# A hybrid stick-breaking and retention step on one core: DRAM read-backs and 32x32 transposes of the first group bound to products in the schedule, the sample row finished apart, value panels moved

## The chip, the cores and the metric

The kernel runs on one core of a Trainium2 chip. The metric is device time of one execution in microseconds (us), the median of several runs. All times of the trace are microseconds from the start of the profiled execution's span. Engines are named as the profile does it: PE multiplies matrices (PEld loads its stationary operand), DVE and ACT are the vector and the scalar engine, POOL is GpSimd, SP only issues DMAs. SPq, ACTq and POOLq are the queues on which an engine issues DMAs.

## What is computed

One layer of a hybrid step over 1,024 prompt rows and a sample of 8 running streams with 16 rows each (128 rows, "the sample row tile"), width 2,048, all in float32:

```python
h = rms_norm(x, norm_pre)
q_sb, k_sb, v_sb, gate_sb, q_r, k_r, v_r, gate_r = split(h @ w_in)    # 8 x 1024 columns, 8 heads of 128
# A: stick-breaking attention, strictly causal
z = q_sb @ k_sb.T / sqrt(128)
log_keep = where(strict, log_sigmoid(-z), 0)
a = where(strict, exp(log_sigmoid(z) + reversed_cumsum(log_keep) - log_keep), 0)
o_sb = a @ v_sb               # sample rows: over 1024 cached keys and values of their stream, then their own
# B: retention with rotary q and k, per-head decay, a state carried over chunks
o_r = decayed(q_r @ k_r.T) @ v_r + decay_read * (q_r @ S);  S = gamma^n * S + (decay_write * k_r).T @ v_r
y = concat(head_rms_norm(o_sb) * silu(gate_sb), head_rms_norm(o_r) * silu(gate_r))
x = x + rms_norm(y @ w_out, norm_post)
```

Outputs are the rows, the new keys and values, and the retention states, for prompt and sample.

## The kernel before

**Products.** Each float32 operand is split into a high part and a rest (`split`, L126: ACT writes the high part `wh`, DVE subtracts to get `wl`), and each product is three matmuls (high x high, high x rest, rest x high). The normed rows stand in SBUF as `mh`, `ml` (the moving operand); the weights stream through: SP loads a 128x512 tile (`wr`), ACT and DVE split it, PE uses it. `wp`, the pool of these tiles, has 4 buffers. A "product" below is one matmul of L206 or L252 (L225 and L274 in the changed file).

**Groups and heads.** The rows are handled in two groups: group 0 holds prompt tiles 0 to 3 and the sample tile (5 tiles of 128 rows, in pieces of 256 and 384), group 1 holds prompt tiles 4 to 7 (one piece of 512). For each of 8 heads the main loop (from L803) emits the projections in this order: `project` of column blocks 4 (retention q) and 5 (retention k), every second head `project_rows` of block 6 (retention v of two heads, "the value panel"), `project` of 7 (retention gate), 0 and 1 (stick-breaking q and k), every second head `project_rows` of 2 (v of two heads), `project` of 3 (gate). After both groups the output projection follows (`out_panel`).

**Side work.** All else is done by generators wrapped in `Job`: `ret_branch` (retention of a head), `sb_branch` (stick-breaking of its prompt rows), `decode` (its sample rows, over the cache). After each product step `tick()` advances one job by one step if its time has come; the number a generator yields is how many ticks it then waits. These numbers are the table `D_*` (first value: group 0, second: group 1). `drain(job)` ticks until a job is done, with no product between the steps. In this way the order of the program is written; a scheduler of the framework then arranges each engine's instructions by that order and the dependences it knows. Names with a number (`wr_10573`) are buffers of the schedule.

**Turning through DRAM.** A block matrix is transposed in two halves: `turn_out` writes it to DRAM (`s_be` and `s_bd` for the weights of stick-breaking of prompt and sample rows, `s_rk` for retention keys, `s_o` for a finished head), `turn_in` (L438) reads it back with the 32x32 blocks in transposed places by four DMAs, and a DVE `transpose` then turns every 32x32 block. Between the halves a job waits `D_TO` ticks (for stick-breaking rows `D_TB` and the steps of the next row), between read-back and transpose `D_TI`.

- `stick_breaking` (L515): step s issues the read-back of row s-1 (POOL's queue) first, then transposes row s-2 (L525), then computes scores, sigmoids and weights of row s and writes them out, then multiplies row s-2 with `vn` (L559).
- `decode` (L566): loads the cached keys of the head in 16 pieces (`kc`, L585, POOL's queue), transposes each on DVE (L610), multiplies; loads the cached values in 8 pieces of 512 KB (`vc`, L616, SP's queue). `kcT` and `vc` share 5 buffers (`V_BUFS`), so piece k+5 is loaded once the matmuls of piece k (L648) are issued. Its last steps copy and combine the accumulator `pa` into tile 4 of `so` on DVE (L654, L656).
- `pa` is the one buffer of the PSUM pool `psa`, shared by L559, L641, L648 and the retention outputs L686, L691.
- `sb_branch` waits at L796 until `decode` is done, then finishes all 5 tiles of the head (`Out.finish`: norm, `turn_out`, `turn_in`, transpose L504, times gate, store to `s_y`).

Of the kernel before, what the change touches and what calls it, by code (L numbers as in the profile page):

```python
# [34 lines left out]
D_NAT = (14, 11)  # L35
# [9 lines left out]
D_TO = (26, 23)  # L45
D_TB = (33, 33)
D_TI = (12, 13)
# [9 lines left out]
def tile_hybrid_step(  # L57
# [88 lines left out]
    phase = [0]  # L146

    class Job:
        def __init__(self, steps, after=0):
            self.steps, self.at, self.done = steps, clock[0] + after, False  # L150
            jobs.append(self)

    def tick():
        clock[0] += 1
        for job in jobs:
            if job.at <= clock[0]:
                wait = next(job.steps, None)
# [43 lines left out]
    def products(mov, acc, pieces, w, wh, wl):  # L201
        hi, lo = mov
        for j in range(WQ):
            for n, (lhs, rhs) in enumerate(((wh, hi), (wh, lo), (wl, hi))):
                for a, (o, m) in zip(acc, pieces):
# [6 lines left out]
                    )  # L212
                tick()
# [15 lines left out]
    def project_rows(g, mov, col, dst, off):  # L229
# [5 lines left out]
        for w in range(KT // 2):  # L235
# [4 lines left out]
            )  # L240
            wh = wp.tile([P, 2, 2 * P], F32R, name="whn", tag="wh")
            wl = wp.tile([P, 2, 2 * P], F32R, name="wln", tag="wl")
            split(wh, wl, wr)
            for j in range(2):
                q, jj = divmod(2 * w + j, WQ)
                for t in range(nt):
                    a = banks[t // 2][:, t % 2, :]
                    ts = slice(t * P, (t + 1) * P)
                    for n, (lhs, rhs) in enumerate(((hi, wh), (hi, wl), (lo, wh))):


                        nc.tensor.matmul(  # L252
# [13 lines left out]
    with ExitStack() as s1:  # L266
# [29 lines left out]

        def ret_inputs(g, mov, h, acc):
            rq = rope(acc, "rq", *ropes)
            rk = rope(project(g, mov, col(5, h)), "rk", *ropes)
            if h % 2 == 0:  # L300
                pair["r"] = ep.tile([P, 5, 2, P], F32, name="rv", tag="rv")
                project_rows(g, mov, col(6, h), pair["r"], 0)
            rv = pair["r"][:, :, h % 2, :]
            return rq, rk, rv, gate(project(g, mov, col(7, h)), "rg")
# [9 lines left out]
        with tc.tile_pool(name="p0", bufs=2) as p0, tc.tile_pool(name="p0s", bufs=1) as p0s, tc.tile_pool(  # L314
# [90 lines left out]
            first = ret_inputs(g0, mov, 0, list(zip(acc, g0["pieces"])))  # L405
            drain(job)
# [31 lines left out]
        def turn_in(s, raw, q):  # L438

            for i in range(4):  # L440
                q.dma_start(  # L441
                    raw[32 * i : 32 * i + 32, :].rearrange("p (k a) -> p k a", a=32),
                    s[:, :, 32 * i : 32 * i + 32].rearrange("k (j b) a -> b (k j) a", b=32),
                )
# [37 lines left out]
        class Out:  # L482
            def __init__(self, g, tag):
                nt = len(g["tiles"])
                self.g, self.nt = g, nt
# [7 lines left out]
            def finish(self, b, h, gT, oT, dst):  # L493
# [4 lines left out]
                s = turn_out(self.o, f"s_o{b}_{h}_{self.nt}")  # L498
# [5 lines left out]
                nc.vector.transpose(oT[:, :n], flat)  # L504
# [10 lines left out]
        def stick_breaking(g, h, out, q2, k2, rest):  # L515
# [3 lines left out]
            for step in range(len(todo) + lag):  # L519
                if 0 < step <= len(todo):  # L520
                    _, be, turned = rows[step - 1]
                    turn_in(turned, be, nc.gpsimd)
                if step >= lag:
                    kp, be, _ = rows[step - lag]
                    nc.vector.transpose(kp[:, : be.shape[1]], be)  # L525
                if step < len(todo):
# [3 lines left out]
                    for s, w in z_pieces(n):  # L530
# [11 lines left out]
                        yield D_ZP[phase[0]]  # L542
                    yield D_TB[phase[0]]
# [525 lines left out]
```

## Time and profile before

| | us |
|---|---|
| runs, median (lowest to highest) | 2468.1 (2465.5 to 2471.39) |
| the profiled execution, own time | 2463.17 |
| its span in the trace | 2461.1 |
| PE busy in the span | 2367.9 |

The profiled execution is one whole run; it lies 4.9 us under the median, and 2.1 us of its own time lie outside the span. PE is busy for 96% of the span. The stages by time: until about 150 us the rows are normed and turned and the first products start; group 0 runs to about 1,120 us; the change of groups, where the side work of group 0's last head meets the first projections of group 1, to about 1,240 us; group 1 to about 2,020 us; then the rest of the output projection. A row of the windows gives, for each engine, busy us with the number of instructions, then the clock that was granted to PE (1.00 is full), the share of the DMA engines' time, and GB/s. A row of the waits gives the waiting engine and line, what released it, the total us, how often, and the longest.

### The profile page before, as it was taken

What the parts mean: (1) busy time and instruction counts of PE and PEld (TensorE: products, weight loads), DVE (VectorE), ACT (ScalarE), POOL (GpSimd) and SP (SyncE); (2) the same over time, 40 slices, a digit from 0 to 9 for tenths busy, and PEclk for the clock granted to TensorE, in tenths of its full rate; (3) what the DMA queues carried; (4) which work ended last, traced back from release to release, by engine and by line L of the source; (5) the groups of instructions that cost most, each with busy time, mean ns of one, the idle gap of its engine ahead of it and who ended that gap; (6) DMA issues with size and microseconds to landing.
All of it is one profiled execution on the core that took longest, in us unless ns stands there. A gap on an engine that the chain in (4) does not pass through costs nothing.

```text
span 2461.1 us, 40322 instructions
## 1 busy us (share of the span) xinstructions
PE 2367.9 (96%) x14832; PEld 2099.4 (85%) x14832; DVE 1250.0 (51%) x2362; ACT 903.8 (37%) x1913; POOL 641.9 (26%) x1029
## 2 busy tenths in 40 slices
PE   7999899999999999998799999999999998999998
PEld 7999888989898888988578898889889886878787
DVE  8245454454444454444545544554564555564544
ACT  6323232333233232233334434344344443444333
POOL 3244354443433344333402111120220211000000
PEclk9999999999999999999999999999999998999999
DMA  7769677695948678495955655665564566665553
GB/s 241 165 144 210 143 191 173 173 199 140 212 125 221 149 177 178 130 226 146 209 161 150 153 152 142 144 163 135 153 160 128 152 152 170 224 221 191 184 184 133
DMA packets 673094, 418.65 MB, mean 170 GB/s; under 512 B 223744, under 2 KB 617984, under 8 KB 670464
## 3 DMA queue, kind: packets, MB, share of 16 engines
q1 hardware_dynamic: 523760, 285.99, 45.9%
q0 software_dynamic: 32256, 71.36, 12.5%
q10 hardware_dynamic: 116880, 58.74, 8.6%
q8 instruction: 116, 1.90, 0.3%
q14 instruction: 82, 0.67, 0.1%
HBM read 336.24 MB, written 79.69 MB: 169 GB/s over the span
## 4 chain that ended last, share of the span: by engine, by line
PE 75%; DMA 10%; issue 9%; DVE 4%; POOL 1%; ACT 1%; SPq 0%; ACTq 0%; DVEq 0%; POOLq 0%
PE acc L206 38%; PE accn L252 14%; PE a L890 4%; PE a L891 4%; PE a L889 4%; PE pa L559 2%; DMA vc<-cache_sb_v 2%; PE z L535 2%; DMA wr<-w_in 1%; PE zc L601 1%; DMA ro<-s_rk 1%; DMA kc<-cache_sb_k 1%; DMA s_rk<-rk 1%; PE pa L648 1%; DMA s_be<-be 1%
## 5 line engine op out<-in xcount | busy, mean ns | idle before, releaser
L206 PE MATMUL acc<-ml,wh 128*128 128x256 f32 (+2 forms) x2304 | 677.0, 343 | 0.2 <-DVE ml L128 0.2
L206 PE MATMUL acc<-mh,wh 128*128 128x256 f32 (+2 forms) x2304 | 670.5, 341 | 6.5 <-ACT rv L262 3.8
L206 PE MATMUL acc<-mh,wl 128*128 128x256 f32 (+2 forms) x2304 | 669.9, 341 | 3.7 <-DVE wl L128 3.7
L128 DVE TENSOR_TENSOR wl<-wr,wh 128x512 fp32r<-128x512 f32 (+1 forms) x576 | 394.7, 691 | 503.5 <-ACT wh L127 498.5
L127 ACT ACTIVATE wh<-wr 128x512 fp32r<-128x512 f32 (+1 forms) x576 | 356.6, 625 | 730.4 <-PE acc L206 367.9
L206 PEld LDWEIGHTS acc<-mh,wh 128*128 128x128 f32 x2304 | 425.3, 189 | 51.3 <-issue 14.3
L206 PEld LDWEIGHTS acc<-mh,wl 128*128 128x128 f32 x2304 | 425.1, 189 | 47.6 <-issue 12.2
L206 PEld LDWEIGHTS acc<-ml,wh 128*128 128x128 f32 x2304 | 422.5, 190 | 40.3 <-issue 12.4
L585 POOL DMA_DIRECT2D kc<-cache_sb_k x512 | 331.4, 653 | 367.8 <-DVE kcT L610 167.5
L252 PE MATMUL accn<-whn,mh 128*128 128x256 f32 x1152 | 332.5, 289 | 0.0
L252 PE MATMUL accn<-wln,mh 128*128 128x256 f32 x1152 | 326.9, 284 | 3.8 <-DVE wln L128 3.8
L252 PE MATMUL accn<-whn,ml 128*128 128x256 f32 x1152 | 326.5, 284 | 0.0
L252 PEld LDWEIGHTS accn<-whn,mh 128*128 128x128 f32 x1152 | 221.2, 192 | 12.9 <-issue 10.8
L890 PE MATMUL a<-wl,mh 128*128 128x512 f32 (+1 forms) x576 | 221.2, 384 | 7.7 <-DVE wl L128 7.7
L252 PEld LDWEIGHTS accn<-wln,mh 128*128 128x128 f32 x1152 | 221.3, 192 | 7.0 <-DVE wln L128 5.5
L252 PEld LDWEIGHTS accn<-whn,ml 128*128 128x128 f32 x1152 | 221.0, 192 | 1.7 <-issue 1.7
L891 PE MATMUL a<-wh,ml 128*128 128x512 f32 (+1 forms) x576 | 220.5, 383 | 0.0
L889 PE MATMUL a<-wh,mh 128*128 128x512 f32 (+1 forms) x576 | 219.3, 383 | 1.0 <-DVE sg L279 0.6
L890 PEld LDWEIGHTS a<-wl,mh 128*128 128x128 f32 x576 | 109.3, 190 | 31.3 <-DVE wl L128 10.6
L127 ACT ACTIVATE whn<-wrn 128x512 fp32r<-128x512 f32 x128 | 79.8, 634 | 151.2 <-PE acc L206 39.8
L441 POOL DMA_DIRECT2D be<-s_be x128 | 94.1, 741 | 142.4 <-DMA s_be<-be 124.0
L128 DVE TENSOR_TENSOR wln<-wrn,whn 128x512 fp32r<-128x512 f32 x128 | 86.8, 687 | 83.4 <-ACT whn L127 82.8
(184 smaller groups left out, 2602.4 us busy)
## 6 DMA issues: line engine op xcount, KB each, us to landing
wr<-w_in SPq DMA_DIRECT2D x384, 256.0 KB, 3.8
wr<-w_out SPq DMA_DIRECT2D x184, 256.0 KB, 3.6
wrn<-w_in SPq DMA_DIRECT2D x128, 256.0 KB, 3.1
kc<-cache_sb_k POOLq DMA_DIRECT2D x512, 64.0 KB, 4.3
vc<-cache_sb_v SPq DMA_DIRECT2D x64, 512.0 KB, 8.7
xt<-x_prompt SPq DMA_DIRECT2D x8, 1024.0 KB, 6.1
xr<-x_prompt SPq DMA_DIRECT2D x8, 1024.0 KB, 6.0
out<-out ACTq DMA_DIRECT2D x12, 512.0 KB, 2.9
```

Of the source, the lines that this page charges most:

```text
L127: nc.scalar.activation(hi, src, AF.Copy)
L128: nc.vector.tensor_tensor(lo, src, hi.bitcast(F32), ALU.subtract)
L206: last = nc.tensor.matmul(a[:, :m], lhs[:, j, :], rhs[w][:, j, o : o + m], start=(w == 0 and j == 0 and n == 0), stop=(w == KT // WQ - 1 a ...
L252: nc.tensor.matmul(a, lhs[q][:, jj, ts], rhs[:, j, :], start=(w == 0 and j == 0 and n == 0 and t % 2 == 0), stop=(w == KT // 2 - 1 and j = ...
L441: q.dma_start(raw[32 * i : 32 * i + 32, :].rearrange("p (k a) -> p k a", a=32), s[:, :, 32 * i : 32 * i + 32].rearrange("k (j b) a -> b (k ...
L535: nc.tensor.matmul(z[:, :c], q2[a][:, i * P : (i + 1) * P], k2[b][:, s : s + c], start=(m == 0), stop=(m == 2),)
L559: nc.tensor.matmul(po[:, :P], at[:, j, :], vn[:, j, :], start=(j == 0), stop=(j == t))
L585: nc.gpsimd.dma_start(kc[32 * i : 32 * i + 32, :].rearrange("p (k d) -> p k d", d=32), cache_k[0, 2 * c + j, s * 512 : (s + 1) * 512, h, 3 ...
L601: nc.tensor.matmul(z[r, :], qp[:, j, r], ready[c // 2][:, c % 2, :], start=(j == 0), stop=(j == 1))
L889: nc.tensor.matmul(a[:, :width], hi[q][:, j, ts], wh, start=(k == 0), stop=False)
L890: nc.tensor.matmul(a[:, :width], hi[q][:, j, ts], wl, start=False, stop=False)
L891: nc.tensor.matmul(a[:, :width], lo[q][:, j, ts], wh, start=False, stop=(k == KT - 1))
```

## The change

It is confined to the side work and to where two kinds of projection panel stand.

1. `tied()` adds, in group 0 only, a dependence for the scheduler alone (no semaphore) from each read-back DMA and each transpose after a read-back to the product that was emitted last (`anchor`).
2. Spacing of group 0: `D_NAT` 14 to 8, `D_TO` 26 to 32, `D_TB` 33 to 17 with a new `D_TA` of 14 ahead, `D_TI` 12 to 32. In `stick_breaking` the read-back of row s-1 moves behind the scores of row s. A job keeps the phase in which it was made, so that group 0's jobs keep their numbers when they run on into group 1.
3. The sample row gets an `Out` of its own (`do`, 128x128) and a job of its own for its finish (norm, write-out, read-back, 128x128 transpose, gate); the finish of the prompt rows covers 4 tiles and no longer waits for `decode`. A `drain(sub)` stands ahead of the next head's `decode` instead.
4. The retention value panel (block 6) moves to the end of the odd head before; in group 1 the panel of head 0 comes first and takes over the loads of its moving rows. `ret_branch` starts ahead of the gate projection 7 and waits for the gate only at its finish.

```diff
-D_NAT = (14, 11)
+D_NAT = (8, 11)
...
-D_TO = (26, 23)
-D_TB = (33, 33)
-D_TI = (12, 13)
+D_TO = (32, 23)
+D_TA = (14, 0)
+D_TB = (17, 33)
+D_TI = (32, 13)
...
+    def tied(ins):
+
+        if phase[0] == 0 and anchor[0] is not None:
+            tc.add_manual_dep(
+                ins.ins,
+                anchor[0].ins.name,
+                mybir.DependencyInfo(mybir.DependencyClass.NoSync, mybir.DependencyReason.SCHED_ONLY),
+                reason="tied to the products",
+            )
...
+                anchor[0] = last
                 tick()
...
-                        nc.tensor.matmul(
+                        anchor[0] = nc.tensor.matmul(
...
+        def ret_values(g, mov, h, loads=None):
+            pair["r"] = ep.tile([P, 5, 2, P], F32, name="rv", tag="rv")
+            project_rows(g, mov, col(6, h), pair["r"], 0, loads)
...
         def turn_in(s, raw, q):
 
             for i in range(4):
-                q.dma_start(
...
+                tied(
+                    q.dma_start(
...
-                nc.vector.transpose(oT[:, :n], flat)
+                tied(nc.vector.transpose(oT[:, :n], flat))
...
-                if 0 < step <= len(todo):
-                    _, be, turned = rows[step - 1]
-                    turn_in(turned, be, nc.gpsimd)
+                early = D_TA[phase[0]] == 0
+
+                def read_back():
+                    if 0 < step <= len(todo):
+                        _, be, turned = rows[step - 1]
+                        turn_in(turned, be, nc.gpsimd)
+
+                if early:
+                    read_back()
                 if step >= lag:
                     kp, be, _ = rows[step - lag]
-                    nc.vector.transpose(kp[:, : be.shape[1]], be)
+                    tied(nc.vector.transpose(kp[:, : be.shape[1]], be))
...
                         yield D_ZP[phase[0]]
+                if not early and step <= len(todo):
+                    yield D_TA[phase[0]]
+                    read_back()
                     yield D_TB[phase[0]]
...
-        def decode(h, out, qs, rest):
+        def decode(h, qs, rest):
             i = 4
+            out = Out(1, "do")
...
-            out.done(i)
+            out.done(0)
+            while "sg" not in rest:
+                yield 3
+            last_row = slice(4 * P, 5 * P)
+            oT = op.tile([P, P], F32, name="doT", tag="doT", bufs=1)
+            Job(out.finish(0, h, rest["sg"][:, last_row], oT, s_y[0][h][:, last_row]))
...
-            while "sg" not in rest or sub is not None and not sub.done:
+            while "sg" not in rest:
...
-                    acc = project(g, mov, col(4, h), loads, (0, 1))
-                    loads = None
+                    if h == 0:
+                        ret_values(g, mov, h, loads)
+                        loads = None
+                    acc = project(g, mov, col(4, h))
                     drain(ret_job)
-                    inputs = ret_inputs(g, mov, h, acc)
+                    inputs = *ret_inputs(g, mov, h, acc), {}
                 ret_job = Job(ret_branch(gi, g, h, *inputs), D_NAT[phase[0]])
+                if "rg" not in inputs[-1]:
+                    inputs[-1]["rg"] = gate(project(g, mov, col(7, h)), "rg")
...
-                out = Out(g, "so")
+                out = Out(4, "so")
                 rest = {}
-                sub = Job(decode(h, out, qs, rest), D_DEC) if SAMPLE in tiles else None
+                if SAMPLE in tiles:
+                    drain(sub)
+                    sub = Job(decode(h, qs, rest), D_DEC)
...
+                if h % 2 and h < H - 1:
+                    ret_values(g, mov, h + 1)
```

How the order of instructions moves is shown at three places. In the rows stand the line in the file concerned, the operation, and destination<-sources.

The first is SP's queue where head 5 of group 0 passes into head 6. `wr` and `wrn` are weights, `vc` the cached values of `decode`, `ro<-s_rk` the read-back of the retention keys, `so<-s_o0` that of the finished stick-breaking tiles. Before:

```order
L441 DMA ro_10779<-s_rk0_6_10781 32x20x32
L616 DMA vc_10421<-cache_sb_v 128x8x128
L616 DMA vc_10469<-cache_sb_v 128x8x128
L192 DMA wr_10645<-w_in 128x4x128
L616 DMA vc_10511<-cache_sb_v 128x8x128
L192 DMA wr_10697<-w_in 128x4x128
L192 DMA wr_10734<-w_in 128x4x128
L192 DMA wr_10768<-w_in 128x4x128
L192 DMA wr_10806<-w_in 128x4x128
L441 DMA ro_10779<-s_rk0_6_10781 32x20x32 x2
```

After:

```order
L654 DMA vc_10738<-cache_sb_v 128x8x128
L654 DMA vc_10768<-cache_sb_v 128x8x128
L211 DMA wr_11100<-w_in 128x4x128
L654 DMA vc_10792<-cache_sb_v 128x8x128
L466 DMA ro_10686<-s_rk0_6_10688 32x20x32 x4
L466 DMA so_9439<-s_o0_5_4_0_10714 32x16x32 x4
L211 DMA wr_11151<-w_in 128x4x128
L211 DMA wr_11192<-w_in 128x4x128
```

The four read-backs of the keys, scattered before, stand together and are followed by the four of the finished tiles; between `wr_11100` and the next weights lie nine DMAs.

The second is DVE where head 6 passes into head 7: L765 (L808 after) transposes the retention keys that were read back, L654 and L656 (L692 and L694) empty the accumulator of `decode`. Before:

```order
L610 STREAM_TRANSPOSE kcT_12573<-kc_12568 128x512
L765 STREAM_TRANSPOSE rkn_12344<-ro_12345 128x640
L279 TENSOR_TENSOR rg_12275<-rg_12275,acc0_12122 128x256
L279 TENSOR_TENSOR rg_12275<-rg_12275,acc1_12123 128x384
L128 TENSOR_TENSOR wl_12406<-wr_12403,wh_12405 128x512
L767 TENSOR_SCALAR rkn_12344<-rkn_12344,dec_76 128x128
L654 COPY so_10878<-pa_12045 128x128
```

After:

```order
L808 STREAM_TRANSPOSE rkn_12278<-ro_12279 128x640
L713 TENSOR_TENSOR sc_12512<-rs_12510,dT_12508 128x128
L810 TENSOR_SCALAR rkn_12278<-rkn_12278,dec_76 128x128
L812 TENSOR_SCALAR rkn_12278<-rkn_12278,dec_76 128x512
L811 TENSOR_SCALAR rkn_12278<-rkn_12278,dec_76 128x128
L648 STREAM_TRANSPOSE kcT_12759<-kc_12754 128x512
L713 TENSOR_TENSOR sc_12547<-rs_12545,dT_12508 128x128
L692 COPY do_11046<-pa_12285 128x128
```

In both the copy out of `pa` stands behind the transpose of the keys. What moved is what the copy is combined into (`do`, a tile of its own, for `so`), and that score rows of the retention (L713) and a piece of cached keys (L648) stand between the two, where gate and weights stood.

The third is PE at the change of groups, where the last pieces of `decode` of head 7 (`vc`) meet the first projections of group 1. Before:

```order
L206 MATMUL acc0_13711<-mh0_12778,wl_13715 128x512
L206 MATMUL acc0_13711<-mh1_12851,wh_13741 128x512
L206 MATMUL acc0_13711<-ml1_12852,wh_13741 128x512
L206 MATMUL acc0_13711<-mh1_12851,wl_13742 128x512
L648 MATMUL pa_13544<-vc_13641,kp_12464 32x256 x4
L206 MATMUL acc0_13711<-mh1_12851,wh_13741 128x512
L206 MATMUL acc0_13711<-ml1_12852,wh_13741 128x512
```

After:

```order
L225 MATMUL acc0_13888<-mh1_13039,wl_13935 128x512
L686 MATMUL pa_13805<-vc_13842,kp_12643 32x256 x4
L744 MATMUL pS_13921<-rv_13106,rkn_13771 128x128
L711 MATMUL rs_13944<-rq_13640,rk_13739 128x128
L744 MATMUL pS_13960<-rv_13106,rkn_13771 128x128
L686 MATMUL pa_13805<-vc_13867,kp_12643 32x256
L711 MATMUL rs_13973<-rq_13640,rk_13739 128x128
L744 MATMUL pS_13995<-rv_13106,rkn_13771 128x128
L686 MATMUL pa_13805<-vc_13867,kp_12643 32x256 x3
L686 MATMUL pa_13805<-vc_13902,kp_12643 32x256 x4
L729 MATMUL pa_13909<-rv_13106,sc_13882 128x128
L734 MATMUL pa_13909<-S_13878,rq_13640 128x128
```

Before, products stand on both sides of a piece (nine between it and the piece ahead); after, the last three pieces and the retention of group 1's head 0 (L711, L744, L729, L734) follow one another without a product.

More of the change, by code (lines that the diff above doesn't have):

```diff
@@ L146, in tile_hybrid_step, with step @@
     phase = [0]
+    anchor = [None]
+    def tied(ins):
[6 more added lines that the diff above has]
+            )
+    def step(job):
+        now, phase[0] = phase[0], job.phase
+        wait = next(job.steps, None)
+        phase[0] = now
+        return wait
     class Job:
@@ L156, in tick @@
             if job.at <= clock[0]:
-                wait = next(job.steps, None)
+                wait = step(job)
                 jobs.remove(job)
@@ L240, in project_rows @@
             )
+            for _ in range(WQ if loads and w in (0, 2) else 0):
+                next(loads)
             wh = wp.tile([P, 2, 2 * P], F32R, name="whn", tag="wh")
```

51 lines of the change are left out of this document (28 added, 23 removed).

## Prediction

> **What bounds the kernel now.** I read the page's head first, then the windows by stage, then the waits of PE in each stage, then what the releasers themselves waited for.
>
> ```profile
> span 2461.1 us, 40322 instructions
> PE 2367.9 (96%) x14832; PEld 2099.4 (85%) x14832; DVE 1250.0 (51%) x2362; ACT 903.8 (37%) x1913; POOL 641.9 (26%) x1029
> ```
>
> The windows (PE is the first pair of busy us and count):
>
> ```profile
> 0.00:150.00 150.00, 134.63 (x991) 132.42 (x992) 77.74 (x177) 70.60 (x127) 42.02 (x64) 0.99 0.72 195
> 150.00:1120.00 970.00, 935.23 (x6810) 853.59 (x6809) 463.87 (x931) 294.34 (x655) 398.50 (x666) 0.99 0.77 174
> 1120.00:1240.00 120.00, 106.41 (x656) 91.13 (x655) 66.08 (x128) 45.80 (x99) 40.27 (x68) 0.94 0.74 181
> 1240.00:2020.00 780.00, 779.18 (x4445) 678.08 (x4444) 410.93 (x732) 312.59 (x649) 127.94 (x200) 1.00 0.58 148
> 2020.00:2461.00 441.00, 412.43 (x1938) 344.20 (x1936) 231.43 (x396) 180.47 (x385) 33.21 (x32) 0.98 0.60 189
> ```
>
> PE bounds it; no other engine passes 51%. The change adds no product, so time can come only from PE's idle time and its clock. PE's idle time by stage is the window less the busy time: 15.4 us at the start, 34.8 in group 0, 13.6 at the change of groups, 0.8 in group 1, 28.6 at the end. The start and the end hold nothing that the change ties or spaces, and group 1 has 0.8 to give. So the question is what becomes of 34.8 and 13.6. The waits of PE in group 0 (waiting line, releaser, total us, times, longest):
>
> ```profile
> PE pa L559 <- DVE so L656: 12.2, 4, 7.5
> PE pa L648 <- DMA vc<-cache_sb_v: 9.8, 5, 4.0
> PE acc L206 <- ACT rv L262: 3.8, 2, 2.3
> PE acc L206 <- DVE wl L128: 3.6, 2, 2.1
> PE zc L601 <- DVE kcT L610: 2.9, 3, 1.6
> PE acc L206 <- ACT vn L262: 1.4, 2, 1.1
> PE pa L641 <- DVE kp L635: 1.1, 1, 1.1
> ```
>
> and at the change of groups its two longest:
>
> ```profile
> PE rs L668 <- DVE rk L290: 5.1, 1, 5.1
> PE accn L252 <- DVE wln L128: 3.0, 1, 3.0
> ```
>
> The first seven add up to 34.8, the whole idle time of group 0. The largest is not what its name says. L656 is a 0.34 us instruction; its longest wait, 7.5 us, looks like this on DVE (first two rows) and PE (third; in square brackets the idle time ahead and its releaser):
>
> ```profile
> 1114.26 0.84 DVE L765 STREAM_TRANSPOSE rkn<-ro 128x640 f32<-128x640 f32 x1 [6.48 <-DMA ro<-s_rk]
> 1117.65 0.34 DVE L656 SCALAR_TENSOR_TENSOR so<-pa,dec,so 128x128 f32<-128x128 f32 x1
> 1118.14 1.62 PE L559 MATMUL pa<-vn,kb 128*128 128x128 f32 x6 [7.47 <-DVE so L656]
> ```
>
> DVE stood 6.48 us on a read-back, the copy that frees `pa` stood behind it in DVE's order, and PE behind that copy. How often DVE stands on read-backs in group 0, and how long a read-back takes (us to landing, last column of the rows of DMAs):
>
> ```profile
> DVE kb L525 <- DMA kb<-s_be: 48.2, 12, 6.0
> DVE rkn L765 <- DMA ro<-s_rk: 14.7, 4, 6.5
> ```
>
> ```profile
> wr<-w_in SPq DMA_DIRECT2D x384, 256.0 KB, 3.8
> vc<-cache_sb_v SPq DMA_DIRECT2D x64, 512.0 KB, 8.7
> s_rk<-rk ACTq DMA_DIRECT2D x8, 320.0 KB, 6.2
> ro<-s_rk SPq DMA_DIRECT2D x32, 80.0 KB, 6.2
> ```
>
> The two groups of waits are 62.9 us on DVE, most hidden, since PE has products to go on with. Idle time is paid a second time through the clock:
>
> ```profile
> 263.40:266.80 3.40, 3.40 (x20) 3.09 (x13) 1.00 (x4) 0.00 (x0) 0.00 (x0) 0.50 1.20 183
> 826.60:830.00 3.40, 0.79 (x7) 0.64 (x6) 3.20 (x10) 0.14 (x1) 0.88 (x2) 1.00 0.67 129
> 830.00:833.40 3.40, 3.40 (x17) 3.40 (x16) 1.22 (x5) 0.41 (x3) 1.58 (x3) 0.50 0.51 116
> 833.40:836.80 3.40, 3.40 (x25) 3.40 (x24) 1.28 (x5) 2.81 (x7) 0.99 (x2) 1.00 0.32 68
> 1113.30:1123.50 10.20, 5.36 (x23) 5.39 (x24) 5.64 (x18) 1.20 (x7) 2.39 (x4) 0.50 0.38 89
> ```
>
> After a 3.4 us stretch in which PE was busy for 0.79, the next ran at 0.50 (17 matmuls) and the one behind it at full clock (25). 3.4 us at half clock cost at most 1.7; I take 1.6. Between 150 and 1,120 us five such stretches stand (the first and the last are shown) and the one at 1113.3, where half of 5.36 busy us, 2.7, is lost: 5 x 1.6 + 2.7 = 10.7 us.
>
> [...]
>
> **The change part by part.**
>
> *Ties and spacing (parts 1 and 2).* In the order, a product being one matmul, the read-back of the keys stands 15 to 106 products behind its write-out before, by the head, and 48 behind it in each head after; the transposes then follow another 16 to 66 behind the last read-back (9 to 44 before). The rows that turn products into time:
>
> ```profile
> 681.75 18.48 PE acc L206 x126
> 1401.85 23.87 PE acc L206 x104
> ```
>
> 0.147 us in group 0, 0.230 in group 1. Fifteen products are 2.2 us, less than the 6.2 us of `s_rk` above, so there the read-back was issued too early and SP waited in it; 48 are 7.1 us, more than 6.2. A gap of 16 to 66 products is 2.3 to 9.7 us against the 6.2 us of the second half, so short gaps still stall DVE, but for the difference only, and the copy of L656 behind waits for that much. Of 12.2 us I leave 1 (bounds: 0, as in group 1, whose whole idle time is 0.8; 12.2 if landings drift as much as spacing grew). The 3.6 on `wl` is DVE late for the same reason: 1 left. The 2.9 on `kcT` waits for `kc` loads from POOL's queue, which still carries 64 KB pieces and read-backs: 2.9 left (0 to 6). The transpose `kp` of the sample row now stands 10 products (1.5 us) ahead of its use: 1.1 becomes 3 (0 to 7 x 1.1 = 8).
>
> *Cached values.* The 9.8 us on `vc` fell where pieces 5 to 7 were issued 15 to 20 products (2.2 to 2.9 us) ahead of use, in heads 0 and 1; the other heads had 67 and more (9.8 us, over the 8.7 to landing). After, head 0 has 30, 41 and 52 products (4.4, 6.0, 7.6 us), heads 1 to 6 have 70 to 88. Three pieces short by up to 4.3, 2.7 and 1.1, where an earlier wait delays the later ones: 3 us left (0 to 8). Head 7 is told below.
>
> *Sample row alone (part 3).* 9 DVE and 4 ACT instructions and 4 read-backs more in each head. The nearest row is L656 above, 128x128, 0.34 us: 9 x 0.34 = 3.1 us of DVE per head of about 120, beside DVE at 48% in this stage. Hidden by products; with that cover gone (a stall of DVE in which PE waits for `wl`) it would cost up to 3.1 x 8 = 24. I take 0. The prompt finish, no longer behind `decode`, starts earlier: this frees `so`, which no PE wait names.
>
> *Value panels and the gate (part 4).* The same matmuls and loads in another place. The 3.8 + 1.4 us on `rv`, `vn` are PE waiting while ACT empties PSUM banks; the panels keep that form: 5.2 left (3 to 8). SP carries the panel's loads past other jobs' read-backs; its weights stay 75 and more products ahead of use (11 us against 3.8 to land), 13 to 51 once, where head 0 passes into head 1. That place may cost up to 2 us; 0 taken.
>
> Group 0: 1 + 3 + 1 + 2.9 + 5.2 + 3 = 16.1, from 34.8: -18.7. Of the six half-clock stretches two stay (head 0's `vc`, one at large), 3 of 10.7: -7.7.
>
> *Change of groups.* Here the order speaks against the change. Three pieces of `decode` of head 7 (L686 on `vc`) are loaded 16, 4 and 0 products ahead of use, where nine products stood between them before; behind them the four steps of the retention of group 1's head 0 follow without a product, each through the one `pa` buffer. What such a step is made of, and what a bare `vc` queue looked like here:
>
> ```profile
> L686 PE MATMUL pa<-rv,sc 128*128 128x128 f32 x64 | 12.3, 275 | 0.0
> L695 DVE SCALAR_TENSOR_TENSOR ro<-pa,dec,ro 128x128 f32<-128x128 f32 x32 | 11.1, 348 | 14.2 <-ACT ro L694 13.8
> ...
> L694 ACT ACTIVATE ro<-pa 128x128 f32<-128x128 f32 x32 | 8.9, 278 | 28.6 <-PE pa L691 28.6
> ```
>
> ```profile
> 1192.90 11.94 SPq L616 DMA_DIRECT2D vc<-cache_sb_v  x5
> ```
>
> The pile: 8.7 for the last `vc` to land, less 16 x 0.230 = 3.7 of products; DVE's copy and two combinations, 3 x 0.34 = 1.0; four steps of two matmuls (0.275 each), L694 (0.278) and L695 (0.348), 1.2 each, 4.7 in all; the next weights' split stands behind the last L694 on ACT, 0.3 at least. Sum 11.0. At the least the loads land as the pile's own matmuls run, 3; at the most all three queue as the five did in 11.94 us and the chain follows whole, 20. I take 11. Of the old 13.6, 9 stay (the `rk` and `wln` waits belong to heads' starts that are kept): 20 for 13.6, +6.4. The longer pile brings one more half-clock stretch, +1.6.
>
> Group 1 and the output panels have almost the same order: 0, within 3 either way. Sum: -18.7 - 7.7 + 6.4 + 1.6 = -18.4 on the profiled execution, 2463.2 to 2444.8. That execution lies 4.9 under the median, so the median to expect is 2449.7; I say 2449.
>
> **The rivals.**
>
> *Smaller gain.* A tie holds the order of a list, no time: with the DMA engines 0.77 busy in group 0 landings spread; those of `ro`, least, median and most:
>
> ```profile
> DMA to landing us min/median/max: 1.9/3.7/13.2
> ```
>
> A transpose whose data comes late still blocks DVE. If half of the two largest waits and of the clock stay, 11 of the 26.4 us are not gained: about 2460. [...]
>
> *The change of groups eats it.* With the pile at its upper end of 20 (+9), clock for two more stretches (+3), and 7 of the gain unrealized: 2468, no change.
>
> *Slower: weights starve behind a run of DMAs on SP.* In each steady head nine DMAs now stand between two weight loads on SP, seen in the order, eight of them read-backs that wait for a write-out to land. SP is in order, and the next weights are used 187 products after the first of those `vc`, 27.5 us. The run decides when it takes longer than 27.5 less 3.8 to land, 23.7 us. What such waits cost SP before:
>
> ```profile
> SPq L441 <- DMA s_bd<-be: 41.0, 7, 9.9
> ```
>
> ```profile
> 1100.21 8.31 SPq L441 DMA_DIRECT2D ro<-s_rk  x4
> ```
>
> Two fours at 8.31 (last row) and one wait of 9.9 are 26.5, over the limit by 2.8; with the mean wait, 41.0/7 = 5.9, they are 22.5 and under it. A stall of 2.8 us with 1.7 of clock in each of seven heads is +32 on the expected time: about 2481. Against it: the four `ro` here were issued into a write-out barely begun, and after the change write-outs are 48 products old.
>
> *More gain.* If `rv`, `kp` and the change of groups cost nothing extra, 8 to 15 us more: 2436.
>
> **How the numbers follow.** A difference of 0.2%, 4.9 us, is about what a measurement of this kernel can tell from none. The forecast (2440 to 2457): 0.53. Smaller gain (2457 to 2463): 0.17. No change (2463 to 2473): 0.13. Slower (above 2473, about 2481): 0.11. More gain (under 2440): 0.06. Faster: 0.53 + 0.17 + 0.06 = 0.76; same 0.13; slower 0.11. The range leaves out the slower case and half of "more gain": 2434 to 2472. The forecast's own range is 2440 to 2457.
>
> **What would show it.** In the trace after: PE's idle time in group 0 near 16 us, the wait on L656's successor (L694) near 1, on `vc` near 3 and only in head 0; no more than two or three stretches at 0.50 there; at the change of groups a run of waits of 5 to 12 us at L686 and L729 with a half-clock stretch behind it; group 1 as it was; SP's weights never named by PE. Wrong it would be if PE waits for `wl` with SP as the root in steady heads, if L525's successor blocks DVE in more than a few heads, or if the pile at the change of groups exceeds 20 us.

## The result, and the profile after

| | before | changed |
|---|---|---|
| median of 7 runs, us | 2469.2 (2464.6 to 2474.4) | 2454.13 (2446.88 to 2463.56) |
| ratio to before | | 0.994, 95% interval 0.9921 to 0.9959 |
| profiled execution, own time | 2463.17 | 2452.19 |

The change gains 15 us, 0.6%; 19 were forecast. The head of the page and the windows, the last one shorter since the span is:

```profile
span 2450.5 us, 40488 instructions
PE 2372.9 (97%) x14832; PEld 2100.2 (86%) x14832; DVE 1263.9 (52%) x2434; ACT 915.1 (37%) x1931; POOL 655.6 (27%) x1029
```

```profile
150.00:1120.00 970.00, 959.98 (x7047) 880.62 (x7047) 489.48 (x1038) 324.74 (x712) 410.23 (x681) 1.00 0.84 178
1120.00:1240.00 120.00, 105.88 (x626) 81.69 (x626) 61.16 (x118) 43.81 (x86) 33.30 (x57) 0.95 0.81 184
1240.00:2020.00 780.00, 766.41 (x4275) 665.62 (x4274) 412.90 (x721) 300.18 (x634) 145.48 (x206) 0.99 0.59 146
2020.00:2450.00 430.00, 406.38 (x1917) 340.40 (x1916) 222.83 (x384) 176.20 (x378) 28.67 (x25) 0.98 0.60 188
```

PE's idle time in group 0's window falls from 34.8 to 10.0 us. In group 1's it rises from 0.8 to 13.6, which the prediction did not have. Windows of fixed times cut the two programs at different work, though. Both issue the same 10,368 product matmuls, so I cut both traces at the same counts: a stage ends where the first product behind a head's gate projection 3 starts. All stage times below are taken so.

| stage | before | changed | difference |
|---|---|---|---|
| until the first product | 22.4 | 25.9 | +3.5 |
| group 0 | 1143.6 | 1110.1 | -33.5 |
| head 0 of group 1 (change of groups) | 156.1 | 163.6 | +7.5 |
| heads 1 to 7 of group 1 | 700.5 | 712.9 | +12.4 |
| from there to the last matmul of the output | 428.2 | 427.7 | -0.5 |

Most of the first row isn't the change: the traces of the twelve runs below give 21.6 to 25.0 us, with this part of the program untouched in all. The rows add up to -10.6 us and the two profiled executions differ by 11.0, where the medians differ by 15.1. Stage times of group 0 with the same instructions there (the changed kernel, e1, e2) lie between 1110.1 and 1113.1, so 3 us is about what a stage of one trace can tell.

The waits of PE in group 0 and, in a second fence, at the change of groups:

```profile
PE acc L225 <- DVE wl L129: 3.2, 2, 2.5
PE pa L729 <- DVE do L694: 3.1, 3, 2.3
PE pa L686 <- DMA vc<-cache_sb_v: 1.5, 2, 1.3
PE zc L639 <- DVE kcT L648: 0.7, 1, 0.7
PE pa L596 <- DVE kb L556: 0.5, 1, 0.5
```

```profile
PE pa L596 <- DVE kb L556: 3.8, 2, 2.5
PE accn L274 <- ACT mh L128: 2.9, 2, 1.8
PE acc L225 <- ACT wh L128: 1.9, 2, 1.8
PE pa L729 <- DVE do L694: 1.8, 1, 1.8
PE pS L744 <- DVE rkn L812: 1.1, 1, 1.1
PE pa L686 <- DMA vc<-cache_sb_v: 1.0, 1, 1.0
```

In group 0 the 12.2 us behind L656 have become 3.1 behind L694, its successor, the 9.8 on cached values 1.5, and the 5.2 on emptied value panels are gone. At the change of groups the forecast pile is there, smaller and spread over more names (6.5 us of waits from 1226.5 to 1243.4 us). Its end on PE:

```profile
1227.62 0.64 PE L686 MATMUL pa<-vc,kp 128*32 128x256 f32 x8 [1.05 <-DMA vc<-cache_sb_v]
...
1239.28 0.79 PE L729 MATMUL pa<-rv,sc 128*128 128x128 f32 x2 [0.75 <-DVE ro L738]
...
1241.25 0.80 PE L729 MATMUL pa<-rv,sc 128*128 128x128 f32 x2 [0.75 <-DVE ro L738]
...
1243.36 0.80 PE L225 MATMUL acc<-mh,wh 128*128 128x512 f32 x1 [0.89 <-ACT wh L128]
```

Cached values, then retention steps about 2 us apart, each waiting for the tile ahead to leave `pa`, then the weights' split on ACT; the clock is at half from 1237.2 to 1247.4:

```profile
1237.20:1247.40 10.20, 7.71 (x22) 5.91 (x23) 4.53 (x17) 6.30 (x20) 0.00 (x0) 0.50 0.22 66
```

The loss in group 1 recurs in each odd head at the same place. On ACT (the first three rows) and PE (the others, not all of its rows), at head 1:

```profile
1369.23 0.36 ACTq L533 DMA_DIRECT2D s_y<-rg  x1
1369.62 1.05 ACTq L825 DMA_DIRECT2D out<-kn  x2
1371.59 1.28 ACT L485 ACT_TABLE_LOAD   x1 [4.47 <-DMA out<-kn]
1371.17 0.34 PE L566 MATMUL z<-kh,ql 128*128 128x384 f32 x1
1372.05 0.29 PE L566 MATMUL z<-kh,ql 128*128 128x256 f32 x1
1372.17 0.39 PE L566 MATMUL z<-kh,qh 128*128 128x512 f32 x1
1373.81 0.39 PE L566 MATMUL z<-kh,qh 128*128 128x256 f32 x1 [0.78 <-ACT be L486]
1376.65 0.50 PE L225 MATMUL acc<-mh,wl 128*128 128x512 f32 x1 [1.04 <-DVE wl L129]
```

The same place of the kernel before, at head 3:

```profile
1600.41 0.34 PE L535 MATMUL z<-kh,ql 128*128 128x384 f32 x1
1600.83 1.28 ACT L459 ACT_TABLE_LOAD   x1 [3.25 <-PE z L535]
1601.28 0.29 PE L535 MATMUL z<-kh,ql 128*128 128x256 f32 x1
1601.41 0.39 PE L206 MATMUL acc<-mh,wh 128*128 128x512 f32 x1
```

The store of the finished retention tiles (`s_y<-rg`) now stands between the four stores of keys on ACT, and ACT is idle for longer ahead of the table load. That is not the loss: in both kernels the table load starts 0.08 us after the scores that its sigmoids read (PE's rows of 384 columns). What differs is PE's own order. Before, 12 products follow the score piece of 256 columns; after, the next row's pieces follow at once, and the second of them has to wait until ACT, behind its table load, is through with the first piece's sigmoids. The weights' split comes late as well. In the four odd heads the two waits come to 7.3 us, and the half-clock stretches behind two of them to 3.4, of the 12.4.

### The profile page after: what moved, and what is told of

The parts are those of the page before. It is cut to its first block, busy times and chain, and to the rows that moved or that the text cites. A ratio compares the mean times of both kernels' runs of the same rounds, so it can differ in the third digit from the quotient of the medians.

```text
span 2450.5 us, 40488 instructions
## 1 busy us (share of the span) xinstructions
PE 2372.9 (97%) x14832; PEld 2100.2 (86%) x14832; DVE 1263.9 (52%) x2434; ACT 915.1 (37%) x1931; POOL 655.6 (27%) x1029
## 4 chain that ended last, share of the span: by engine, by line
PE 70%; issue 12%; DMA 8%; DVE 6%; POOL 2%; ACT 1%; SPq 1%; DVEq 0%; ACTq 0%; POOLq 0%
PE acc L225 33%; PE accn L274 15%; PE a L944 4%; PE a L945 4%; PE a L943 4%; PE pa L596 2%; DMA kc<-cache_sb_k 2%; DMA wr<-w_in 1%; PE z L566 1%; PE zc L639 1%; POOL kc L623 1%; DMA mr<-s_y 1%; PE pa L686 1%; DMA ro<-s_rk 1%; DVE wl L129 1%
## 5 line engine op out<-in xcount | busy, mean ns | idle before, releaser
L225 PE MATMUL acc<-mh,wl 128*128 128x256 f32 (+2 forms) x2304 | 661.5, 340 | 7.4 <-DVE wl L129 7.4
L225 PE MATMUL acc<-ml,wh 128*128 128x256 f32 (+2 forms) x2304 | 666.8, 342 | 0.0
L225 PEld LDWEIGHTS acc<-mh,wh 128*128 128x128 f32 x2304 | 419.2, 189 | 54.4 <-issue 16.6
L274 PEld LDWEIGHTS accn<-whn,mh 128*128 128x128 f32 x1152 | 219.8, 191 | 18.7 <-issue 11.7
L491 POOL TENSOR_SCALAR_AFFINE_SELECT kp<-kp 128x128 f32<-128x128 f32 x40 | 12.4, 311 | 472.2 <-ACT kp L485 472.1
```

Source lines behind the costliest of these rows:

```text
L225: last = nc.tensor.matmul(a[:, :m], lhs[:, j, :], rhs[w][:, j, o : o + m], start=(w == 0 and j == 0 and n == 0), stop=(w == KT // WQ - 1 a ...
L274: anchor[0] = nc.tensor.matmul(a, lhs[q][:, jj, ts], rhs[:, j, :], start=(w == 0 and j == 0 and n == 0 and t % 2 == 0), stop=(w == KT // 2 ...
```

## The experiments

The theory at this point: group 0's gain is made by spacing and ties, group 1's loss by the retention job that now starts ahead of the gate projection (through its last store on ACT, which the rows above do not bear out), the loss at the change of groups by the value panel that goes first there. Stages of all runs (us), and the ratio to the kernel before, run beside each (medians of 2468.3 to 2473.2), with its interval:

| run | group 0 | change of groups | group 1, heads 1 to 7 | median | ratio |
|---|---|---|---|---|---|
| e1 | 1112.1 | 158.4 | 701.6 | 2435.14 | 0.9862 (0.9838 to 0.9887) |
| e2 | 1113.1 | 153.0 | 701.1 | 2426.5 | 0.9828 (0.9804 to 0.9852) |
| e3 | 1109.6 | 162.8 | 714.9 | 2450.23 | 0.9918 (0.9886 to 0.9949) |
| e4 | 1129.3 | 152.5 | 711.5 | 2458.72 | 0.9952 (0.9937 to 0.9968) |
| e5 | 1118.5 | 150.8 | 700.1 | 2434.39 | 0.9864 (0.9846 to 0.9882) |
| e6 | 1148.3 | 172.3 | 700.5 | 2484.22 | 1.0065 (1.0048 to 1.0082) |
| e7 | 1131.5 | 144.5 | 700.2 | 2442.4 | 0.9895 (0.9877 to 0.9914) |
| e8 | 1111.2 | 159.3 | 700.5 | 2438.06 | 0.9879 (0.9859 to 0.99) |
| e9 | 1149.7 | 159.9 | 700.5 | 2474.42 | 1.0 (0.9985 to 1.0016) |
| e10 | 1144.1 | 172.7 | 700.5 | 2481.99 | 1.004 (1.0023 to 1.0057) |
| e11 | 1110.1 | 151.6 | 700.2 | 2429.22 | 0.9824 (0.9808 to 0.9841) |
| e12 | 1122.1 | 153.8 | 701.1 | 2438.4 | 0.9872 (0.9853 to 0.9892) |

**e1: the retention job late again, in group 1 only.**

```diff
+                if gi == 1:
+                    inputs[-1]["rg"] = gate(project(g, mov, col(7, h)), "rg")
                 ret_job = Job(ret_branch(gi, g, h, *inputs), D_NAT[phase[0]])
```

> Changed kernel, but in group 1 the retention job starts behind the gate projection again (part 4 undone in that point for group 1). Theory A: the loss in group 1 (heads 1 to 7 took 700.5 us before, 712.9 after) comes from the earlier retention job, whose last store falls on ACT's queue between the key stores and the first sigmoid. Then heads 1 to 7 of group 1 take 700 to 704 us, no PE wait for the score buffers is left there, and the whole is 9 to 13 us under the changed kernel, about 0.989 of the kernel before. Rival B: the moved value panel makes the loss: 710 to 714 us in those heads, 0.994 of before. Group 0 as in the changed kernel (1110 us), change of groups (head 0 of group 1) 160 to 165 us by both.

Theory A holds as to the part: heads 1 to 7 of group 1 take 701.6 for 712.9, and 19 us of the median go, more than the 9 to 13 expected. Its reason does not, as the rows above show: what the late job brings back is the products between the score pieces (24 at head 1, 12 at the other odd heads), and both waits are gone. Why the framework's scheduler packs the pieces when the job is early stays open. The change of groups fell too, by 5, which neither theory had.

**e2: group 1 written as before.** On e1, the value panel of group 1 behind the key projection again, in place of the end of the head before.

```diff
-                    if h == 0:
-                        ret_values(g, mov, h, loads)
...
-                    acc = project(g, mov, col(4, h))
+                    acc = project(g, mov, col(4, h), loads, (0, 1))
...
+                    if gi == 1 and h % 2 == 0:
+                        ret_values(g, mov, h)
...
-                if h % 2 and h < H - 1:
+                if gi == 0 and h % 2 and h < H - 1:
```

> As the run before, and in group 1 the value panel stands behind the key projection again, with the loads of the moving rows in the first projection: group 1 is written as in the kernel before. Theory A: heads 1 to 7 of group 1 as in the run before (700 to 703 us). Rival B: only here do they fall from 712 to 701. For the change of groups (156.1 us before, 163.6 after): if the pile of cached values and retention steps comes from the group-1 panel that went first, it falls to 154 to 158; if it comes from group 0's longer spacing running on into group 1, it stays at 161 to 166. Whole: 2433 to 2445, 0.986 to 0.990 of before.

The change of groups takes 153.0, 3 less than before the change, so group 0's longer spacing alone makes no pile; it takes the panel that went first and the early job, and, as e4 below shows, the longer spacing with them. With 2426.5 us this is the fastest kernel here by its median: 1.7% under the kernel before, where the whole change gives 0.6%.

**e3: no ties.**

```diff
-        if phase[0] == 0 and anchor[0] is not None:
+        if False:
```

> Changed kernel without the dependences of read-backs and transposes on products; spacing and all else as changed. Theory T (the ties make the gain of group 0, 1143.6 to 1110.1 us, since without them the scheduler moves read-backs off the places that the spacing gives them): group 0 takes 1125 to 1145 us, total 2468 to 2488. Rival S (spacing and the moved read-back make it): group 0 1108 to 1116, total within 5 us of the changed kernel, 2449 to 2459.

Theory T falls: group 0 takes 1109.6 without a single tie. The order does change (84 of SP's 1,239 DMAs stand outside the longest order that both traces share), and DVE stands on read-backs of other kinds: 26.2 us on `s_be`, where the changed kernel has 7.9, and none on `s_rk`, where that has 24.5. PE takes no harm of it:

```profile
DVE kb L556 <- DMA kb<-s_be: 26.2, 10, 4.9
```

**e4: ties kept, group 0's spacing as before.**

```diff
-D_NAT = (8, 11)
-D_TO = (32, 23)
-D_TA = (14, 0)
-D_TB = (17, 33)
-D_TI = (32, 13)
+D_NAT = (14, 11)
+D_TO = (26, 23)
+D_TA = (0, 0)
+D_TB = (33, 33)
+D_TI = (12, 13)
```

> Changed kernel with group 0's old spacing (14, 26, 33, 12, and read-backs ahead of the next row's scores), ties kept. Theory T: group 0 1110 to 1120 us, total 2452 to 2464. Rival S: group 0 1125 to 1145 us, total 2467 to 2487, with DVE's longest waits on read-backs back at 5 us and more.

In group 0 the spacing is worth 19 of the 33.5 us. What came back is not DVE on `s_be` but cached values and, behind DVE's transposes of the retention keys, `rkn`:

```profile
PE pa L686 <- DMA vc<-cache_sb_v: 19.9, 14, 2.6
PE pS L744 <- DVE rkn L812: 10.0, 5, 4.0
```

At the change of groups the old spacing gains 11 (152.5 for 163.6, with panel and early job as changed), so the total misses rival S's range and lies in theory T's, and the interval of its ratio overlaps that of the changed kernel. Of the 19 us, the longer spacing loses 11 again in the next stage.

**e5: sample row within the head's finish (part 3 undone on e2).**

```diff
-                out = Out(4, "so")
+                out = Out(nt, "so")
...
-            while "sg" not in rest:
+            while "sg" not in rest or sub is not None and not sub.done:
```

> Base: the run e2 (changed kernel with group 1 written as before; group 0 takes 1113 us, total 2426.5). Undone on it: part 3, so the sample row is tile 4 of the finished head again, and the finish waits for the sample row's job. Of the 33 us that group 0 gained, old spacing gave back 19, ties 0; 14 must come from parts 3 and 4. Theory P3: the sample row gives them, since the finish of a head then waits for the last cached values and its read-backs fall into the next head: group 0 takes 1122 to 1128 us, total 2435 to 2442. Rival P4: group 0 stays at 1111 to 1116, total 2424 to 2430.

Between the two: group 0 loses 5.4 us (1118.5) and gets 2 back at the change of groups; the median rises by 8. The sample row's own finish costs nothing and gains a little. By which way isn't shown: PE's idle time in group 0 is 13.2 us here and 11.9 in e2.

**e6: part 4 undone in group 0 too (on e2).**

```diff
-                    if gi == 1 and h % 2 == 0:
+                    if h % 2 == 0:
                         ret_values(g, mov, h)
...
-                if gi == 1:
+                if (gi, h) != (0, 0):
                     inputs[-1]["rg"] = gate(project(g, mov, col(7, h)), "rg")
...
-                if gi == 0 and h % 2 and h < H - 1:
-                    ret_values(g, mov, h + 1)
```

> Base as the run before (e2), undone: part 4 in group 0 as well, the value panel behind the key projection and the retention job behind the gate projection. P4: group 0 takes 1120 to 1128 us (the waits on the panel's emptied banks, rv, 3.8 us before and none after, come back, with half-clock stretches), total 2434 to 2442. P3: 1111 to 1116 us, total 2424 to 2430.

P4 holds as to the part, and by far more than expected: group 0 takes 1148.3, as if nothing had been changed, the change of groups 172.3, and the kernel is 0.65% slower than the one before. Its reason falls: no wait on `rv` came back. PE waits for cached values and for weights instead:

```profile
PE pa L686 <- DMA vc<-cache_sb_v: 13.8, 8, 3.2
PE acc L225 <- ACT wh L128: 13.5, 6, 3.1
```

**e7 and e8: the spacing split (on e2).** e7 has `D_TO = (26, 23)`, `D_TI = (12, 13)`; e8 has `D_NAT = (14, 11)`, `D_TA = (0, 0)`, `D_TB = (33, 33)`.

> Base e2 with D_TO and D_TI of group 0 as before (26 and 12 for 32 and 32; write-out to read-back, read-back to transpose of retention keys, sample row and finished heads). If the late cached values of the run with all old spacing (15 waits of PE, one or two in each head) come from these two, since the sample row's matmuls then start 26 ticks sooner while its loads do not: group 0 takes 1124 to 1132 us, with waits on cached values in every head; if from the row spacing: 1111 to 1117. Total by the first 2437 to 2446, by the second 2425 to 2431.

> Base e2 with D_NAT, D_TA, D_TB of group 0 as before (14, read-back of a row ahead of the next row's scores, 33). If the cached values come from D_TO and D_TI: group 0 1111 to 1118 us, no wait on cached values beyond head 0, total 2425 to 2432. If the rows make the loss of the old spacing: 1124 to 1132, total 2437 to 2446.

In group 0 `D_TO` and `D_TI` are the whole of it: e7 loses 18.4 us, e8 none. (2.5 of the 18.4 are one stall on the border; cut ahead of it, e7's stages are about 1129 and 147.) PE's longest waits in group 0 of e7, for 2.0 and none in e2:

```profile
PE pa L686 <- DMA vc<-cache_sb_v: 19.6, 12, 4.0
PE pa L596 <- DVE so L599: 8.0, 5, 2.4
```

The rows' spacing, with the read-back moved behind the next row's scores, is worth nothing in group 0. But e8's median is 12 us above e2's and missed its expectation; its change of groups takes 6 us more, which I didn't resolve.

**e9: the kernel before, with ties alone.** `tied()` around its read-backs and transposes.

> Kernel before with part 1 alone: read-backs and transposes of group 0 depend on the last product in the schedule; all else as before. The run without ties showed that they are worth nothing on top of the other parts. If they are worth something where the spacing is the old one: group 0 takes 1125 to 1138 us (1143.6 before), total 2450 to 2463. If they are worth nothing there either: 1140 to 1147, total within 4 us of the kernel before, 2464 to 2473.

Ratio 1.0: the ties gain no time there either; group 0 takes 1149.7, 6 us more than before and outside both forecasts. Yet on DVE they do what they were meant to: its 48.2 us of waits on `s_be` fall to 1.7, those on `s_rk` from 14.7 to none, and PE's 12.2 us behind L656 are gone. PE waits elsewhere instead, for cached values (9.8 before) and for weights (none before):

```profile
DVE kb L537 <- DMA kb<-s_be: 1.7, 1, 1.7
PE pa L660 <- DMA vc<-cache_sb_v: 22.2, 13, 2.8
PE acc L217 <- ACT wh L127: 6.0, 2, 4.3
```

**e10 and e12: the two halves of part 4 in group 0 (on e2).** e10 starts the retention job of group 0 behind the gate projection again and leaves the panel moved; e12 puts the panel back and leaves the job early.

```diff
 # e10
-                if gi == 1:
+                if (gi, h) != (0, 0):
                     inputs[-1]["rg"] = gate(project(g, mov, col(7, h)), "rg")
 # e12
-                    if gi == 1 and h % 2 == 0:
+                    if h % 2 == 0:
                         ret_values(g, mov, h)
...
-                if gi == 0 and h % 2 and h < H - 1:
-                    ret_values(g, mov, h + 1)
```

> Base e2 (group 1 as before; group 0 1113 us, total 2426.5), undone: the retention job of group 0 starts behind the gate projection again; the value panel stays at the end of the odd head. With both undone group 0 took 1148.3 us. If the earlier retention job makes that difference (its four read-backs and the finished tiles leave SP's queue before the cached values of the sample row are asked for): 1138 to 1150 us, total 2460 to 2476. If the panel does: 1111 to 1118 us, total 2425 to 2432.

> Base e2 (group 0 1113 us, total 2426.5), undone: the value panel of group 0 stands behind the key projection as before, while the retention job still starts ahead of the gate projection. With the job late, group 0 took 1144 us (panel moved) and 1148 us (panel back). If the early job alone opens the gain: group 0 1112 to 1120 us, total 2426 to 2436. If it needs the moved panel, since the panel's 240 products otherwise stand between queries and job: 1130 to 1148, total 2445 to 2475.

The early job is what opens the gain: without it group 0 takes 1144.1 and the change of groups 172.7, and the median, 2482, is above the range expected. The panel adds 9 us (1122.1 without it, between the two forecasts of e12). What the late job does, on SP, ACT and PE of e10:

```profile
768.92 3.61 SPq L654 DMA_DIRECT2D vc<-cache_sb_v  x1
772.62 10.13 SPq L466 DMA_DIRECT2D ro<-s_o  x4
782.87 1.80 SPq L654 DMA_DIRECT2D vc<-cache_sb_v  x2
784.76 11.66 SPq L211 DMA_DIRECT2D wr<-w_in  x4
```

```profile
800.35 0.63 ACT L128 ACTIVATE wh<-wr 128x512 fp32r<-128x512 f32 x1 [10.08 <-DMA wr<-w_in]
```

```profile
801.03 0.90 PE L225 MATMUL acc<-mh,wh 128*128 128x256 f32 x2 [8.19 <-ACT wh L128]
```

The read-back of the finished retention tiles falls among the loads of cached values. The first three of its issues take 2.2 to 2.8 us each, the fourth stands until a cached-values load has landed at 782.44, and from 761 to 785 us SP issues no weights. The first weights after that land 15.6 us after their issue, against a median of 4.6 in this stage: one stall of 8.19 us. Such waits on `wh` come to 24.5 us in group 0 of e10, and there are none in e2. That is the prediction's slower rival, in another version of the kernel, though not by its price: no read-back waits for a write-out here, and it is the landing that is long. In e2 the same read-back stands ahead of all cached values, with weights between:

```profile
743.32 6.21 SPq L466 DMA_DIRECT2D ro<-s_o  x4
749.63 3.83 SPq L211 DMA_DIRECT2D wr<-w_in  x4
753.55 6.59 SPq L654 DMA_DIRECT2D vc<-cache_sb_v  x3
```

From the second head on, the stretch without weights around this read-back lasts 4 to 6 us in e2 and in the changed kernel; from the third on it lasts 21 to 23 in e10. In the kernel before it is as long from the third head on, 20 to 23 us, but the weights behind it land within 9.5, and PE has no wait on `wh` in group 0. So e10's loss is not the old loss come back. Each of these runs takes one part out of e2, and the losses in group 0 (31 for the job, 18.4 for `D_TO` and `D_TI`, 9 for the panel, 5 for the sample row) add up to twice the gain: the parts need each other. The early job alone on the kernel before was not run.

**e11: only the last head of group 0 with the old `D_TO` and `D_TI` (on e2).** A third value in each table, used by the jobs of head 7.

> Base e2, only the jobs of group 0's last head use the old D_TO and D_TI (26 and 12). With these for all heads the change of groups took 144.5 us for 153.0, but group 0 1131.5 for 1113.1. If the last head's jobs alone make the former: change of groups 143 to 148, group 0 1112 to 1117, total 2418 to 2424, the best of all. If it hangs on the heads ahead: 151 to 156, total 2424 to 2430.

The change of groups stays at 151.6; the median, 2429.22, can't be told from e2's. So the 144.5 us of e7 do not come from the last head's numbers alone; that they hang on what the heads ahead leave over is likely, not shown.

## Why the prediction was right, and where it was wrong

The time lies 5 us above the forecast and well within its own range. That it lies so near is in part luck, since two errors of opposite sign meet: group 0 gains 7.1 us more than the 26.4 forecast, and group 1 loses 12.4 that were put at 0.

- *Group 0, -18.7 of idle time and -7.7 of clock.* Too small, and by the wrong part. Between the same products the trace shows -33.5: PE's idle time there is 36.9 us before and 12.4 after, and half of its busy time in the stretches at 0.50, which is what I estimate they cost (after 1377.2 us products started 0.43 us apart there, against 0.23 at full clock), 12.9 and 3.4. The waits left were estimated at 16.1 and are 10.0 in the window. The 12.2 behind L656 left 3.1 (1 forecast), the cached values 1.5 (3), the panels 0 (5.2).
- *The step "ties and spacing".* Its first half holds only for the ties alone: in e9 all waits of DVE on read-backs (`s_be`, `s_o`, `s_bd`, `s_rk`) come to 5.2 us, where the kernel before has 93.0. With the other parts they are 52.0 us with ties and 41.8 without (e3). Its second half, from DVE's waits to PE's time, fails: e9 gains nothing, since PE then waits elsewhere, and e3 loses nothing. The rows' spacing is worth nothing in group 0 (e8). Of the spacing `D_TO` and `D_TI` count, 18.4 us (e7), and mostly through cached values, which my working had put at 6.8.
- *The step "value panels and the gate", taken as 0 in group 0.* This is the one that failed most: "the same matmuls and loads in another place" looked only at the panels' banks. The job that starts 48 ticks earlier is what keeps read-backs out of the cached values' place on SP; with the other parts in, it is worth 31 us in group 0 and 20 at the change of groups (e10 against e2).
- *"Group 1 ... 0, within 3 either way".* Wrong: +12.4. The early job isn't limited to group 0, so it also moved in group 1, where nothing was idle. e1 takes it back to 701.6.
- *The change of groups, +8.* Right in its number, +7.5, but not in its split: idle time rose by 3.2 us for 6.4, and the half-clock loss from 2.8 to 9.0 for 1.6 more; cached values cost 1.0 at the last piece, not 5. It takes group 1's panel and early job together with group 0's longer spacing: e2 takes away the former, e4 the latter, and 153.0 and 152.5 us are left.
- *The sample row at 0.* Near: 5 us of gain in group 0, 8 of the median (e5).
- *The rivals.* "Slower" named the right queue and, as to weights behind read-backs on SP, the right mechanism, but in the changed kernel the run of DMAs stays under its cover (no wait of PE in group 0 goes back to `wh`, the first thing made of a late weight tile); e10 shows what it does when a read-back comes there too early. "The change of groups eats it" fell, since the pile kept to its estimate; "smaller gain" fell for group 0. Its own sum was off: half of what it names is (11.2 + 6.8 + 7.7) / 2 = 12.9 us, not 11, which is 2462, still in its band.

## What to carry to other kernels

SP issued one DMA after another in these rows, and where a read-back stood bore on when the weights behind it went out and landed: in e10 SP issued none from 768.92 to 784.76 us, and PE then stood for 8.19. So ask, for each moved job, which of its DMAs will be slow and what stands behind them. A wait that goes away is not yet time gained: in e9 DVE's waits and PE's longest stall went, and PE waited as long for something else. The idle time ahead of an instruction is not yet a cause either: see when its operands were ready, as with the table load above. Cut two traces at equal counts of work before comparing them: windows of time showed 24.8 us less idle time in one stage and 12.8 more in another, where the stages gained 33.5 and lost 12.4. And when a change holds several parts, apply it only to the stage that has idle time: here the stage that was full lost as much as a third of the gain, and leaving it alone makes 0.6% into 1.7%.

## What the runs showed of the hardware

The same pair of short stalls halves PE's clock in one place and not in another. In the changed kernel, heads 1 and 3 of group 1, the stretch with the stalls and the one behind it:

```profile
1373.60:1377.20 3.60, 2.33 (x8) 1.38 (x9) 2.77 (x3) 3.60 (x9) 0.56 (x2) 0.99 0.00 0
1377.20:1380.60 3.40, 3.40 (x9) 2.65 (x8) 3.40 (x5) 0.80 (x4) 1.90 (x3) 0.50 0.67 199
1584.40:1588.00 3.60, 2.34 (x8) 1.38 (x9) 2.78 (x3) 3.60 (x10) 0.56 (x2) 1.00 0.00 0
1588.00:1591.40 3.40, 3.40 (x16) 2.82 (x15) 3.40 (x5) 1.32 (x4) 1.89 (x3) 1.00 0.64 195
```

PE was busy for 2.33 and 2.34 of 3.60 us; only the first was followed by 0.50, with 9 matmuls where the other did 16. The stalls are the same in both, 0.78 and 1.04 us, and no single wait there was longer. Nor does busy time alone tell such places apart in this trace. Ahead of the 12 half-clock stretches that start between 150 and 2,100 us, PE was busy for 0.94 to 2.28 of the last 3.41 us (2.28 ahead of the one at 1377.2). Yet after 1.64 of the 3.41 us that end at 2182.70, the next 3.4 us ran at full clock:

```profile
2179.29:2182.70 3.41, 1.64 (x8) 1.02 (x7) 3.29 (x3) 0.30 (x1) 0.41 (x1) 1.00 0.76 299
2182.71:2186.11 3.40, 2.72 (x11) 1.91 (x11) 2.00 (x1) 2.41 (x4) 2.39 (x1) 1.00 0.90 270
```

What decides between the two was not shown.
